# A two-block transformer kernel: the modulation's sums over partitions by a GpSimd all-reduce and a diagonal picked on VectorE, in place of TensorE's transposes and ones

## The chip, the cores and the metric

One core of one Trainium2 chip runs the program. The metric is device microseconds of one execution, the median of several runs; the profile is of one more execution, taken by the hardware profiler.

## What is computed

The reference is a chain of two transformer blocks on 256 tokens of width 1024, all in float32. The first has a forgetting attention with a convolution beside it and a SwiGLU; the second has two layers (a block attention, a differential attention), each with a SwiGLU, and each modulated by a vector `c`. The change touches only that modulation:

```python
def second_block(x, c, rel_bias, ada_w, ada_b, norm_g, ...):
    c_act = jax.nn.silu(c)
    for i in range(DEPTH_2):
        mod = (c_act @ ada_w[i] + ada_b[i])[:, None, :]
        sh_a, sc_a, g_a, sh_f, sc_f, g_f = jnp.split(mod, 6, axis=-1)
        h = rms_norm(x, norm_g[i, 0]) * (1.0 + sc_a) + sh_a
        ...
        x = x + g_a * rms_norm(y, norm_g[i, 1])
        h = rms_norm(x, norm_g[i, 2]) * (1.0 + sc_f) + sh_f
        x = x + g_f * rms_norm(swiglu_2(h, ffn_w_in[i], ffn_w_out[i]), norm_g[i, 3])
```

`mod` is a product of one row of 1024 numbers with a matrix of 1024 x 6144, twice: 48 MB of weights for one row.

## The kernel before, in words

**Products.** TensorE does every large product in three passes of fp32r: each weight unit of 128 x 512 is split into a high and a low part (`hi` or `wp` by ScalarE, `lo` or `wp` by VectorE, in `fill`, lines 316 to 345), each activation as well, and `triple` (line 370) issues high x high, high x low and low x high. A feed-forward step (`up`, `down`, lines 1089 to 1108) takes eight units up and four down; between them `activate` (line 1069) makes `ep` on VectorE (line 1073: silu times the other half, which lies in a PSUM bank), TensorE turns it (line 1078, matmul `bank<-ident,ep`), and ScalarE and VectorE split it into `pair`.

**The order.** The order of all engines is written by a planner that runs while the program is built (class `Order`, line 108). Its clock, `o.now`, advances with TensorE's matmuls. Small tasks are generators that yield the planner's time at which their next piece may be issued; `pump` runs those that are due between two matmuls. `Lane` (line 74) pins every instruction of an engine behind the one before it and charges it a planned cost. So each engine works through a fixed list, and an instruction that waits holds up everything behind it on its engine. While the chain from one stage to the next is under way (`chain`, line 526; its reciprocal square roots are `pow` on GpSimd, `rstd`, line 485), `o.urgent` is set and optional work is held back.

**The modulation.** `ada` (lines 630 to 661) spreads that product thinly over the first two thirds of the program. For each of 24 sums (two layers, six parts, two halves `cc` of 512 columns) GpSimd clears a tile `asum` (two of them, line 237), a DMA puts the bias into its first partition, and VectorE adds eight weight tiles, each scaled by its partition's number of `c_act` (line 656). What is left is a tile of 128 x 512 whose column sums over the 128 partitions are the result. `ada_finish` (lines 597 to 628) takes that sum:

- For the shifts and scales (`sh_a`, `sc_a`, `sh_f`, `sc_f`: 16 sums) the result must lie along partitions, as `fm`. TensorE turns the tile in four blocks into a bank (line 617), and VectorE sums over the free axis (line 622).
- For the gates (`g_a`, `g_f`: 8 sums) it must lie in every partition. ScalarE and VectorE split the tile (`split`, line 604, into a pair of the weight slots), TensorE multiplies both parts with a matrix of ones (lines 608 and 609), and VectorE multiplies the bank into `gain` (line 613).

The shifts and scales are needed by `evacuate` in the chains, the gates by `scaled_y` (line 533).

Of the kernel before, what the change touches and what calls it, by code (L numbers as in the profile page):

```python
# [5 lines left out]

# [5 lines left out]

# [3 lines left out]
OP = mybir.AluOpType  # L16
AX = mybir.AxisListType
# [3 lines left out]
P = 128  # L21
# [13 lines left out]
ADA_START, ADA_EARLY, ADA_LATE = 30.0, 5.5, 8.0  # L35
HEADS_1, HEADS_2 = 9.0, 2.0
PAD_END = 104
LAG = 3


# [33 lines left out]
class Lane:  # L74
# [7 lines left out]
    def __getattr__(self, name):  # L82
        fn = getattr(self.eng, name)

        def call(out, *args, after=0.0, **kw):
            self.order.pin(self, fn(out, *args, **kw))  # L86
            n = math.prod((args[0] if name == "reduce_sum" else out).shape[1:])
            aps = sum(hasattr(v, "shape") for v in (*args[1:], kw.get("scale"), kw.get("bias"), kw.get("accum_out")))
            cost = self.fixed + self.per * n
            src = args[0] if args and hasattr(args[0], "tensor") else None  # L90
            if src is not None and src.tensor.name.startswith("bank"):
                cost -= 0.042 if name == "activation" else 0.0
            elif name == "tensor_scalar":
                cost -= self.per * n / 2
            if name == "activation":
                cost += 0.093 * aps
            elif name in ("tensor_scalar", "scalar_tensor_tensor"):
                cost += 0.06 * (aps - (name[0] == "s"))
            if name == "activation" and args[1] not in (AF.Copy, AF.Square, AF.Identity, AF.Abs) and args[1] != self.table:
                self.table = args[1]  # L100
                cost += 1.3
            start = max(self.free, after, self.order.now)
            self.free = start + cost
            return self.free + 0.15
        return call
# [107 lines left out]
def block_kernel(ctx: ExitStack, tc: tile.TileContext, a: dict, onehot: bass.AP, out: bass.AP):  # L213
    nc = tc.nc
    o = Order(tc)
    A, V, G = o.A, o.V, o.G
# [6 lines left out]
    def ring(pool, name, n, shape, dtype=F32):  # L223
        return Ring([pool.tile(shape, dtype, name=f"{name}{i}") for i in range(n)])

    def small(name, shape, dtype=F32):
        return cst.tile(shape, dtype, name=name)

    banks = ring(psum, "bank", 8, [P, 512])
    raws = ring(cst, "raw", 3, [P, 2048])  # L230
    araws = ring(cst, "araw", 2, [P, 1024])
    slots = Ring([(small(f"hi{i}", [P, 512], F32R), small(f"lo{i}", [P, 512], F32R)) for i in range(16)])
    st = ring(cst, "st", 4, [P, 528])
# [3 lines left out]
    asum = ring(cst, "asum", 2, [P, 512])  # L237
# [26 lines left out]
    def ffn_stream(w_gu, w_dn, where):  # L264
# [3 lines left out]
        def up(s):  # L268
            for k0 in (0, 4):
                stream.append(Raw(gu[:, k0:k0 + 4, :, s * 256:(s + 1) * 256], 4, 512, where))  # L270

        def down(s):
            stream.append(Raw(dn[:, 2 * s:2 * s + 2, :], 2, 1024, where))
# [3 lines left out]
        for s in range(2, STEPS - 1):  # L277
            up(s)
            if s - 1 < STEPS - LAG:
                down(s - 1)  # L280
        up(STEPS - 1)
        for s in range(STEPS - LAG, STEPS):
            down(s)
# [63 lines left out]
    def split(hi, lo, src, after=0.0):  # L347
        t = A.activation(hi, src, AF.Copy, after=after)
        return V.tensor_sub(lo, src, hi.bitcast(F32), after=t)

    def take(n):
        got = [u for r in stream[pos["use"]:pos["use"] + n] for u in r.units]
        pos["use"] += n
        return got
# [27 lines left out]
    def product(ps, pair, h, ks, us, marks=None, first=True, last=True):  # L382

        n = len(us)
        for i, (k, u) in enumerate(zip(ks, us)):
            if marks is not None:
                o.wait(marks[h][k // 4])
            c = slice(h * P, (h + 1) * P)
            t = triple(ps, pair[0][:, k, c], pair[1][:, k, c], u, first and i == 0, last and i == n - 1)
        return t  # L390
# [71 lines left out]
    ident = small("ident", [P, P])  # L462
# [3 lines left out]
    ones_r = small("ones_r", [P, P], F32R)  # L466
# [130 lines left out]
    def ada_finish(l, what, cc, sums, r):  # L597
        yield r
        c = slice(cc * 512, (cc + 1) * 512)
        if what[0] == "g":  # L600
            yield from o.until(gated[l, what].load)
            pair = yield from o.get(slots)
            hv, lv = pair
            r = split(hv, lv, sums)
            asum.give(sums, r)
            yield r
            tp = yield from o.get(banks)
            o.mm(tp, ones_r, hv, True, False)
            r = o.mm(tp, ones_r, lv, False, True)
            slots.give(pair, r)  # L610
            yield r
            dst = gated[l, what].tile[:, c]
            r = V.tensor_mul(dst, dst, tp)
        else:
            tp = yield from o.get(banks)
            for j in range(4):
                r = o.tr(tp[:, j * P:(j + 1) * P], sums[:, j * P:(j + 1) * P], ident)
            asum.give(sums, r)
            yield r
            i = {"sh_a": 0, "sc_a": 1, "sh_f": 2, "sc_f": 3}[what]  # L620
            dst = fm[l][:, i, cc * 4:cc * 4 + 4]
            r = V.reduce_sum(dst, tp.rearrange("p (k c) -> p k c", c=P), axis=AX.X)
            if what[1] == "c":
                yield r
                g = vec["g", l, 0 if what == "sc_a" else 2][:, cc * 4:cc * 4 + 4]
                r = V.scalar_tensor_tensor(dst, dst, 1.0, g, op0=OP.add, op1=OP.mult)
        banks.give(tp, r)
        ada_done[l, what][cc].t = r

    def ada():  # L630
# [33 lines left out]
    def scope(**kinds):  # L664

        stack, got = ExitStack(), {}
        for name, (n, shape, dtype) in kinds.items():
            got[name] = ring(stack.enter_context(tc.tile_pool(name=name, bufs=1, reuse_waits="tile")), name, n, shape, dtype)
        return stack, got
# [87 lines left out]

    small("pad_end", [P, PAD_END])
    phase, sc = scope(qp=(4, [P, 4, 256], F32), gp=(8, [P, 512], F32),
# [195 lines left out]
    for k0 in (0, 4):  # L955
        for h in range(2):
            t = product(fb[h][:, :260], hT, h, range(k0, k0 + 4), us_f[k0:k0 + 4], hm, k0 == 0, k0 == 4)
# [50 lines left out]
    for n in range(2):  # L1008
        us = take(1)
        o.wait(ya_mark)  # L1010
        for h in range(2):
            ps = o.hold(banks)
            t = product(ps, yaT, h, range(4), us)
# [22 lines left out]
    for h in range(2):  # L1036
        for n in range(2):
            ps = o.hold(banks)
            t = product(ps, ybT, h, range(4), ub[n])
# [23 lines left out]
    def ffn(hm, gb, **kw):  # L1063
# [25 lines left out]
        def up(s, h):  # L1089
            if s not in us_of:  # L1090
                us_of[s] = take(2)
            act_mark[s, h] = Mark()
            ps = o.hold(banks)
            t = product(ps, hT, h, allk, us_of[s], hm)
            o.spawn(activate(s, h, ps), t)
# [14 lines left out]
        def downs(s):  # L1110
            for h in range(2):
                for n in range(2):
                    down(s, h, n)
# [6 lines left out]
        for s in range(2, STEPS - 1):  # L1120
            up(s, 0)
            up(s, 1)
            if s - 1 < STEPS - LAG:
                downs(s - 1)
        us_of[STEPS - 1] = take(2)
        for s in range(STEPS - LAG, STEPS):
            dn[s] = take(1)
        for h in range(2):
            up(STEPS - 1, h)
            o.spawn(chain(h, ys[h], gb, out_marks, **kw))  # L1130
            for s in range(STEPS - LAG, STEPS):
                for n in range(2):
# [237 lines left out]
```

## Time and profile before

| | us |
|---|---|
| median of 3 runs | 990.28 (989.15 to 990.47) |
| the profiled execution | 993.5 |
| its span, first to last instruction | 991.6 |
| TensorE busy | 975.9 of the span |
| VectorE busy | 739.2 |
| ScalarE busy | 605.2 |
| GpSimd busy | 35.2 |

Busy times are unions of an engine's instructions; matmuls are pipelined, and their ends are modelled, so two neighbours overlap. The distance from one start to the next is what a matmul costs in a row of matmuls. "Idle before" is what the engine stood still ahead of an instruction, with what released it. GpSimd's spans are rough.

### The profile page before, as it was taken

The page shows a single profiled execution, that of the slowest core. Times are in us where ns is not written, and L with a number is a line of the kernel's source. Part 1 is how long each engine was busy: PE and PEld are TensorE (multiplying, and loading weights), DVE is VectorE, ACT ScalarE, POOL GpSimd, SP SyncE. Part 2 cuts the span into 40 slices and gives each one's busy share as a digit, 9 for nine tenths or more (in the row PEclk, how much of TensorE's full clock was granted, in tenths as well). Part 3 has the DMA queues.
Part 4 walks back from the last instruction along what each step waited for, and adds up shares of the span by engine and source line. Part 5 has one row for each costly group of instructions (what it writes and reads, how often), then busy time and mean ns, then how long its engine had stood idle before and what let it go on. Part 6 is the DMA issues. An engine that isn't in the chain of part 4 may idle for free.

```text
span 991.6 us, 14032 instructions
## 1 busy us (share of the span) xinstructions
PE 975.9 (98%) x4814; PEld 808.5 (82%) x4814; DVE 739.2 (75%) x1469; ACT 605.2 (61%) x1286; POOL 35.2 (4%) x65
## 2 busy tenths in 40 slices
PE   7999999999999999999999999999999999999997
PEld 6888778888888888898788888888897888888886
DVE  5897879889888958887799888747765786464632
ACT  6746666774555537866685454637788795464531
POOL 1000000000000001000000000001000100000000
PEclk9999999999999999999999999999999999999999
DMA  6969778679989875775759989645542567646401
GB/s 217 361 202 308 254 263 271 218 231 319 363 287 326 294 257 189 253 258 173 233 187 313 369 274 314 231 138 194 176 163 86 172 206 253 211 157 207 163 33 43
DMA packets 143539, 227.19 MB, mean 229 GB/s; under 512 B 5991, under 2 KB 78932, under 8 KB 143468
## 3 DMA queue, kind: packets, MB, share of 16 engines
q1 hardware_dynamic: 143452, 226.30, 68.0%
q8 instruction: 37, 0.61, 0.2%
q14 instruction: 34, 0.28, 0.1%
q10 hardware_dynamic: 16, 0.00, 0.0%
HBM read 225.22 MB, written 2.63 MB: 230 GB/s over the span
## 4 chain that ended last, share of the span: by engine, by line
PE 92%; DMA 3%; issue 2%; DVE 1%; ACT 1%; SPq 0%; POOL 0%; DVEq 0%; POOLq 0%; ACTq 0%
PE bank L140 87%; PE bank L146 5%; DMA raw<-in_w_in_dram 1%; DMA raw<-in_ffn_w_in_dram 1%; DMA araw<-in_ada_w_dram 1%; DVE lo L86 1%; DMA ep<-in_norm_g_dram 0%; SPq L134 0%; DVE asum L86 0%; ACT hi L86 0%; DVE x L86 0%; ACT junk L86 0%; POOL tiny L86 0%; DVE wp L86 0%; DVE ep L86 0%
## 5 line engine op out<-in xcount | busy, mean ns | idle before, releaser
L86 DVE TENSOR_TENSOR lo<-raw,hi 128x512 fp32r<-128x512 f32 (+1 forms) x499 | 322.8, 676 | 41.4 <-ACT hi L86 40.1
L86 ACT ACTIVATE hi<-raw 128x512 fp32r<-128x512 f32 (+1 forms) x499 | 298.0, 620 | 61.4 <-PE bank L140 33.1
L140 PE MATMUL bank<-hi,hTh 128*128 128x512 f32 (+1 forms) x672 | 263.6, 392 | 0.0
L140 PE MATMUL bank<-hi,hTl 128*128 128x512 f32 (+1 forms) x672 | 262.6, 391 | 0.0
L140 PE MATMUL bank<-lo,hTh 128*128 128x512 f32 (+1 forms) x672 | 262.2, 390 | 0.3 <-DVE lo L86 0.3
L140 PE MATMUL bank<-hi,pair 128*128 128x512 f32 x524 | 173.9, 396 | 0.0
L86 DVE SCALAR_TENSOR_TENSOR asum<-araw,c_act,asum 128x512 f32<-128x512 f32 x192 | 143.0, 745 | 7.5 <-DMA araw<-in_ada_w_dram 6.5
L140 PEld LDWEIGHTS bank<-hi,hTl 128*128 128x128 f32 x672 | 126.9, 189 | 25.5 <-issue 1.7
L140 PEld LDWEIGHTS bank<-lo,hTh 128*128 128x128 f32 x672 | 127.0, 189 | 24.0 <-DVE lo L86 0.6
L140 PEld LDWEIGHTS bank<-hi,hTh 128*128 128x128 f32 x672 | 127.1, 189 | 23.3 <-issue 0.2
L140 PE MATMUL bank<-wp,hTh 128*128 128x512 f32 x384 | 119.1, 391 | 0.0
L140 PEld LDWEIGHTS bank<-hi,pair 128*128 128x128 f32 x524 | 98.1, 189 | 19.5
L86 ACT ACTIVATE wp<-raw 128x512 fp32r<-128x512 f32 x145 | 88.5, 629 | 26.0 <-PE bank L140 16.7
L140 PE MATMUL bank<-lo,pair 128*128 128x512 f32 x262 | 103.9, 396 | 0.0
L86 ACT ACTIVATE ep<-bank 128x256 f32<-128x256 f32 x66 | 25.3, 383 | 125.8 <-PE bank L140 125.4
L86 DVE TENSOR_TENSOR wp<-raw,wp 128x512 fp32r<-128x512 f32 x145 | 94.9, 684 | 9.1 <-ACT wp L86 8.3
L140 PEld LDWEIGHTS bank<-wp,hTh 128*128 128x128 f32 x384 | 71.8, 188 | 15.0
L86 DVE TENSOR_TENSOR ep<-ep,bank 128x256 f32<-128x256 f32 x70 | 29.1, 416 | 70.8 <-ACT ep L86 70.2
L140 PE MATMUL bank<-wp,pair 128*128 128x512 f32 x294 | 76.7, 395 | 0.0
L140 PE MATMUL bank<-wp,hTl 128*128 128x512 f32 x192 | 75.1, 391 | 0.0
L140 PEld LDWEIGHTS bank<-wp,pair 128*128 128x128 f32 x294 | 54.3, 188 | 10.9
L86 ACT ACTIVATE pair<-bank 128x256 fp32r<-128x256 f32 (+1 forms) x74 | 28.8, 389 | 53.7 <-PE bank L146 42.4
(128 smaller groups left out, 952.4 us busy)
## 6 DMA issues: line engine op xcount, KB each, us to landing
araw<-in_ada_w_dram SPq DMA_DIRECT2D x96, 512.0 KB
raw<-in_ffn_w_in_dram SPq DMA_DIRECT2D x88, 512.0 KB
raw<-in_w_gate_up_dram SPq DMA_DIRECT2D x44, 512.0 KB
raw<-in_ffn_w_out_dram SPq DMA_DIRECT2D x22, 1024.0 KB
raw<-in_w_in_dram SPq DMA_DIRECT2D x18, 1024.0 KB
raw<-in_moba_w_qkv_dram SPq DMA_DIRECT2D x12, 1024.0 KB
raw<-in_diff_w_qkv_dram SPq DMA_DIRECT2D x12, 1024.0 KB
raw<-in_w_down_dram SPq DMA_DIRECT2D x11, 1024.0 KB
```

Source lines behind the costliest of these rows:

```text
L86: self.order.pin(self, fn(out, *args, **kw))
L140: self.pin(self.pe, self.nc.tensor.matmul(out, lhsT, rhs, start=start, stop=stop, skip_group_check=shared))
L146: self.pin(self.pe, self.nc.tensor.transpose(out, src, ident))
```

## The change

The cross-partition sum leaves TensorE. GpSimd's `partition_all_reduce` writes the column sums of the tile into every partition of a tile of the ring `st` (four tiles, line 233). For the gates VectorE multiplies that into `gain`. For the shifts and scales four VectorE instructions, one for each block of 128 columns, multiply the block with the identity and accumulate along the row, which leaves in partition p the sum of column p. The planner charges the new instruction 8.0 us, and neither it nor the VectorE instructions behind it are issued while `o.urgent` is set.

```diff
-from concourse import mybir
+from concourse import bass_isa, mybir
...
+ALL_REDUCE = 8.0
...
             cost = self.fixed + self.per * n
             src = args[0] if args and hasattr(args[0], "tensor") else None
+            if name == "partition_all_reduce":
+                cost = ALL_REDUCE
...
     def ada_finish(l, what, cc, sums, r):
         yield r
         c = slice(cc * 512, (cc + 1) * 512)
+        while o.urgent:
+            yield o.now + 0.2
+        total = yield from o.get(st)
+        t = total[:, :512]
+        r = G.partition_all_reduce(t, sums, channels=P, reduce_op=bass_isa.ReduceOp.add)
+        asum.give(sums, r)
+        yield r
+        while o.urgent:
+            yield o.now + 0.2
         if what[0] == "g":
             yield from o.until(gated[l, what].load)
-            pair = yield from o.get(slots)
-            hv, lv = pair
-            r = split(hv, lv, sums)
-            asum.give(sums, r)
-            yield r
-            tp = yield from o.get(banks)
-            o.mm(tp, ones_r, hv, True, False)
-            r = o.mm(tp, ones_r, lv, False, True)
-            slots.give(pair, r)
-            yield r
             dst = gated[l, what].tile[:, c]
-            r = V.tensor_mul(dst, dst, tp)
+            r = V.tensor_mul(dst, dst, t)
         else:
-            tp = yield from o.get(banks)
-            for j in range(4):
-                r = o.tr(tp[:, j * P:(j + 1) * P], sums[:, j * P:(j + 1) * P], ident)
-            asum.give(sums, r)
-            yield r
             i = {"sh_a": 0, "sc_a": 1, "sh_f": 2, "sc_f": 3}[what]
             dst = fm[l][:, i, cc * 4:cc * 4 + 4]
-            r = V.reduce_sum(dst, tp.rearrange("p (k c) -> p k c", c=P), axis=AX.X)
+            for j in range(4):
+                r = V.scalar_tensor_tensor(t[:, j * P:(j + 1) * P], t[:, j * P:(j + 1) * P], 1.0, ident, op0=OP.mult, op1=OP.mult,
+                                           accum_out=dst[:, j:j + 1])
...
-        banks.give(tp, r)
+        st.give(total, r)
         ada_done[l, what][cc].t = r
```

On GpSimd, behind the fifth of the 24 sums, where the first projection's four `pow` stand (`tiny<-tiny,mhalf`; `MEMSET asum` clears a sum's tile), the order before is:

```order
L86 MEMSET asum_121 128x512
L86 MEMSET asum_122 128x512
L86 TENSOR_TENSOR tiny_147<-tiny_148,mhalf 128x1
L86 TENSOR_TENSOR tiny_150<-tiny_151,mhalf 128x1
L86 TENSOR_TENSOR tiny_153<-tiny_154,mhalf 128x1
L86 TENSOR_TENSOR tiny_156<-tiny_157,mhalf 128x1
L86 MEMSET asum_121 128x512
```

Nothing stands there but the clears and the `pow`. Now there is also the all-reduce (`ISA st<-asum`, and an `ISA` without tiles, which loads another library of GpSimd code):

```order
L87 MEMSET asum_122 128x512
L87 ISA st_108<-asum_121 128x512
L87 ISA
L87 TENSOR_TENSOR tiny_147<-tiny_148,mhalf 128x1
L87 TENSOR_TENSOR tiny_150<-tiny_151,mhalf 128x1
L87 TENSOR_TENSOR tiny_153<-tiny_154,mhalf 128x1
L87 TENSOR_TENSOR tiny_156<-tiny_157,mhalf 128x1
L87 MEMSET asum_121 128x512
L87 ISA
L87 ISA st_111<-asum_122 128x512
```

Each of the 24 sums has such an all-reduce, and for all but the last two a clear of the same tile waits behind it; a library load stands at each of the eight changes between all-reduces and `pow`, in front of the next instruction that needs it.

On VectorE, in the first modulated feed-forward (the sixth sum, `asum_122`), what stands behind the sum's last addition is now:

```order
L87 SCALAR_TENSOR_TENSOR asum_122<-araw_75,c_act,asum_122 128x512
L87 TENSOR_TENSOR lo_99<-raw_71,hi_98 128x512
L87 TENSOR_TENSOR lo_101<-raw_71,hi_100 128x512
L87 TENSOR_TENSOR lo_103<-raw_71,hi_102 128x512
L87 TENSOR_TENSOR ep_118<-ep_118,bank_65 128x256
L87 TENSOR_TENSOR lo_105<-raw_71,hi_104 128x512
L87 TENSOR_TENSOR lo_107<-raw_72,hi_106 128x512
```

The weight splits `lo<-raw,hi` read two SBUF tiles each; `ep`, which TensorE turns next, is one of a list in which they come first. The sum's diagonal stands sixteen instructions behind that last addition:

```order
L87 TENSOR_TENSOR ep_115<-ep_115,bank_69 128x256
L87 SCALAR_TENSOR_TENSOR asum_121<-araw_75,c_act,asum_121 128x512
L87 SCALAR_TENSOR_TENSOR st_111,fm_191<-st_111,ident 128x128 x4
L87 TENSOR_TENSOR pair_166<-bank_63,pair_166 128x256
L87 TENSOR_TENSOR wp_1634<-raw_73,wp_1633 128x512
```

Before, one `TENSOR_REDUCE fm<-bank` stood four rows behind the sum's last addition. On TensorE the rows `bank<-ident,asum` (16 groups of four) and `bank<-hi,ones_r`, `bank<-lo,ones_r` (8 of each) are gone, and nothing has come in their place.

## Rows read from the trace of the kernel before

**Rows 1.** The page: busy time by engine, and the granted TensorE clock in 40 slices.

```profile
PE 975.9 (98%) x4814; PEld 808.5 (82%) x4814; DVE 739.2 (75%) x1469; ACT 605.2 (61%) x1286; POOL 35.2 (4%) x65
...
PEclk9999999999999999999999999999999999999999
```

**Rows 2.** The page: the chain that ended last, shares by engine.

```profile
PE 92%; DMA 3%; issue 2%; DVE 1%; ACT 1%; SPq 0%; POOL 0%; DVEq 0%; POOLq 0%; ACTq 0%
```

**Rows 3.** Busy time by stretch: stretch, its length, then each engine's.

```profile
40.00:200.00 160.00, 159.66 (x769) 128.74 (x768) 137.03 (x279) 101.97 (x210) 5.83 (x13) 1.00 0.77 259
200.00:372.00 172.00, 171.99 (x793) 140.66 (x792) 146.04 (x255) 89.76 (x172) 4.83 (x10) 1.00 0.88 297
372.00:480.00 108.00, 108.00 (x632) 94.87 (x631) 86.65 (x181) 78.64 (x175) 4.42 (x7) 1.00 0.67 221
480.00:640.00 160.00, 157.57 (x714) 128.71 (x713) 134.05 (x240) 93.08 (x182) 5.93 (x10) 0.99 0.82 278
```

**Rows 4.** Groups by line: busy us, mean ns, idle before (the parts removed).

```profile
L86 DVE TENSOR_REDUCE fm<-bank 128x4 f32<-128x512 f32 x16 | 11.0, 685 | 2.4 <-PE bank L146 2.3
...
L146 PE MATMUL bank<-ident,asum 128*128 128x128 f32 x64 | 9.6, 273 | 0.0
...
L86 DVE TENSOR_TENSOR lo<-asum,hi 128x512 fp32r<-128x512 f32 x8 | 5.5, 692 | 4.5 <-ACT hi L86 4.5
...
L140 PE MATMUL bank<-hi,ones_r 128*128 128x512 f32 x8 | 3.5, 439 | 0.0
```

**Rows 5.** Timeline of PE: start, us, instruction (a shift's four turns; a gate's ones).

```profile
217.86 0.39 PE L140 MATMUL bank<-lo,pair 128*128 128x512 f32 x1
...
218.31 0.60 PE L146 MATMUL bank<-ident,asum 128*128 128x128 f32 x4
...
219.21 0.63 PE L140 MATMUL bank<-hi,pair 128*128 128x512 f32 x2
...
277.81 0.39 PE L140 MATMUL bank<-hi,ones_r 128*128 128x512 f32 x1
...
278.27 0.40 PE L140 MATMUL bank<-hi,hTh 128*128 128x512 f32 x1
```

**Rows 6.** Groups on DVE, shapes apart: the nearest instructions to a diagonal's.

```profile
L86 DVE DVE_READ_ACCUMULATOR2_ANT tiny<- 128x1 f32 x64 | 5.3, 82 | 0.0
...
L86 DVE SCALAR_TENSOR_TENSOR ep<-ep,tiny,ep 128x128 f32<-128x128 f32 x8 | 2.8, 346 | 0.2
```

**Rows 7.** Groups on POOL, shapes apart.

```profile
L86 POOL TENSOR_TENSOR tiny<-tiny,mhalf 128x1 f32<-128x1 f32 x22 | 15.3, 694 | 454.1 <-DVE tiny L86 454.1
L86 POOL MEMSET asum<- 128x512 f32 x24 | 12.6, 525 | 353.9 <-PE bank L146 196.4 <-DVE lo L86 120.4 <-DVE ep L86 18.8
L86 POOL TENSOR_TENSOR tiny<-tiny,mhalf 128x4 f32<-128x4 f32 x4 | 4.3, 1080 | 85.1 <-DVE tiny L86 79.9 <-ACT wp L86 5.1
```

**Rows 8.** Timelines of POOL and DVE around three of the `pow`.

```profile
183.63 0.55 POOL L86 TENSOR_TENSOR tiny<-tiny,mhalf 128x1 f32<-128x1 f32 x1 [43.92 <-DVE tiny L86]
187.43 0.93 POOL L86 TENSOR_TENSOR tiny<-tiny,mhalf 128x1 f32<-128x1 f32 x1 [3.24 <-DVE tiny L86]
...
183.47 0.69 DVE L86 TENSOR_TENSOR ch<-bank,gain 128x512 f32<-128x512 f32 x1
...
187.27 0.68 DVE L86 TENSOR_TENSOR lo<-raw,hi 128x512 fp32r<-128x512 f32 x1
...
498.75 0.68 DVE L86 TENSOR_TENSOR wp<-raw,wp 128x512 fp32r<-128x512 f32 x1
...
498.38 0.55 POOL L86 TENSOR_TENSOR tiny<-tiny,mhalf 128x1 f32<-128x1 f32 x1 [8.24 <-DVE tiny L86]
```

**Rows 9.** Timelines of DVE and PE: an activation made, and turned.

```profile
248.34 0.41 DVE L86 TENSOR_TENSOR ep<-ep,bank 128x256 f32<-128x256 f32 x1
...
248.81 0.44 PE L146 MATMUL bank<-ident,ep 128*128 128x128 f32 x2
```

**Rows 10.** Groups on DVE in the stretch of 200 to 372 us.

```profile
L86 DVE TENSOR_TENSOR ep<-ep,bank 128x256 f32<-128x256 f32 x21 | 8.7, 415 | 9.4 <-ACT ep L86 9.4
```

## The prediction

> **What bounds the kernel now.** [...] The chain that ended last is TensorE for 92% [rows 2]. Then the stretches in which the 24 sums are taken: from 40 to 640 us TensorE is busy 597.2 of 600 us, so a matmul taken away there shortens the program. In the same four stretches VectorE is busy 86, 85, 80 and 84% [rows 3]: not the bound, but with only 15% to spare, a loss on it is won back slowly.
>
> **What it removes.** A shift's four turns: from one matmul to the next but three around them TensorE takes 219.21 - 217.86 = 1.35 us, in which four large matmuls also start; those cost 0.23 each, as the two of the ones do (278.27 - 277.81 = 0.46) [rows 5]. That leaves 0.43 for the turns, 16 x 0.43 = 6.9 us. A gate's ones: 8 x 0.46 = 3.7 us. Together **10.6 us of TensorE**, on the path. Off it go 11.0 us of VectorE's row sums and 5.5 of its splits [rows 4] and as many splits of ScalarE's, which is far from full [rows 1].
>
> **What it adds on VectorE.** A diagonal takes four instructions of 128 x 128 with two SBUF inputs and an accumulator to read; the nearest rows are 346 ns for such a multiply and 82 for the read [rows 6], at most 4 x 0.43 = 1.7 us where one sum took 0.69. So 16 x 1.0 = 16 us more, 5.5 less for the splits: some 10 us in 600. The price lies between nothing (VectorE has the room) and all of it (TensorE reads what VectorE has just made: `ep` ends at 248.75, and its turn starts at 248.81 [rows 9]); I take **2 us**, near the lower end, since the order was written with these instructions in it.
>
> **What it adds on GpSimd.** 24 all-reduces of 128 x 512. No row has one. The nearest below is the clear of as many columns, 0.53 us; the nearest above is `pow`, whose step from one column to four, (1080 - 694) / 3 = 129 ns a column, would give 66 us [rows 7]. The order gives it room: 13 to 17 VectorE instructions stand between nearly every sum's last addition and what reads its all-reduce (sixteen in the order shown), and with its idle time VectorE spends 172 / 255 = 0.67 us on each [rows 3]; so 9 us pass, at the least, before anything on VectorE waits. I take 8 us, the figure the order was laid out for; it is no row's, and what the sum needs of it is first whether it is under 9. Under 9, and if VectorE went on undisturbed, the whole would be 10.6 - 2 = 8.6 us faster. The `pow` of the chains are not behind an all-reduce in time: GpSimd stood idle for 43.9 us ahead of the first of them [rows 8]. The library loads lie in that idle time; ahead of an all-reduce a load would have to take over 1 us to be felt, four times.
>
> **What decides it.** Does a GpSimd instruction that reads SBUF for microseconds let VectorE work? Two sorts of `pow` in the trace say how the two engines share. At 183.63 the `pow` runs beside a multiply that reads a bank and one SBUF tile, and takes 0.55 us. At 187.43 it runs beside a split `lo<-raw,hi`, which reads two SBUF tiles and ends at 187.95; now it takes 0.93 and ends 0.41 later, at 188.36 [rows 8]. So GpSimd's read of a single column waited until the whole VectorE instruction was through: the two do not share column by column, one has the port and the other stands. In the other direction the rows say less: at 498.75 a split starts 0.37 us into a `pow` of 0.55 and takes its usual 0.68 [rows 8], so GpSimd gives the port back at the latest after two thirds of its instruction. A `pow` of one column reads for too short a time to be seen holding anything; an all-reduce reads 512. The hold is thus between nothing and, by two thirds, 0.67 x 8 = 5.4 us. I take 5.4, because the pattern that the rows do show is the exclusive one, and an instruction that sums as it reads has no reason to be done reading early.
>
> What 5.4 us of a standing VectorE cost: behind the sum's last addition stand splits with two SBUF inputs, and `ep` behind them in the list. TensorE's weights are split well ahead, but `ep` is not: it is used 0.06 us after it is made [rows 9]. There are 21 `ep` in 172 us [rows 10], one every 8.2, so the next comes on average 4.1 us after the hold begins, late by the hold less what VectorE wins back until then, 15% of 4.1 = 0.6. Off goes another 0.7, while VectorE finishes the instruction that has the port, and 0.5 for those `ep` that are made earlier than needed. 5.4 - 1.8 = 3.6 us for each of 24, **86 us**.
>
> **The sum**, against the profiled execution's own 993.5 us: 993.5 - 10.6 + 2 + 86 = 1070.9. That execution is 3.2 us above the median shown; against the median it is 990.3 - 10.6 + 2 + 86 = **1068 us**.
>
> **The rivals.**
> - *No hold that matters.* The instruction takes its 512 columns in quickly, or GpSimd is served between VectorE's instructions, as the `pow` at 187.43 was; VectorE never stands. For it: no row shows VectorE held, and clears of 128 x 512 cost VectorE nothing visible (though they do not read). Then 990.3 - 8.6 = 982 us, faster. It decides below a hold of 1.8 + 8.6 / 24 = 2.2 us; just about there the two cancel.
> - *The port is held for the whole instruction.* 24 x (8.0 - 1.8) = 149 us, 990.3 - 8.6 + 149 = 1131 us. The split at 498.75, which started before the `pow` had ended and lost nothing [rows 8], speaks against it, if weakly. [...]
> - *The instruction is longer than its room.* Each microsecond beyond 9 makes the diagonal wait, and VectorE with it, 24 us a microsecond. Of each wait 1.1 us is again won back or covered. At 14 us, 24 x (5 - 1.1) = 94, and without any hold 990.3 - 8.6 + 94 = 1076; gain and loss cancel at 9 + 1.1 + 8.6 / 24 = 10.5. Late clears then also hold the bias DMAs on SP's queue, with the weights behind them. The `pow` price of 66 us would add 24 x (57 - 1.1) = 1,340. [...]
>
> That the change does not do what it says is excluded on TensorE: the turns and the ones are gone from its list.
>
> **How the numbers follow.** About 0.2%, 2 us, is what a measurement of this kernel tells from no change. Forecast (a hold of 2.6 to 6 us): 0.38. No hold that matters: 0.36. Whole instruction: 0.12. Longer than its room: 0.10. Holds that just cancel the gain: 0.04. So faster 0.36, same 0.04, slower 0.60. The forecast's own range is 1001 to 1083 us (holds of 2.6 and 6). The range that is to hold 8 of 10 must take in the rival on the other side, 982 with the whole price of the diagonals' 0 to 10 us open, so from 977; above, it goes to 1128, which leaves out most of the whole-instruction case and the longest instructions.
>
> **What would show it.** If I am right: the group of `lo<-raw,hi`, 0.68 us each now, has members of several microseconds, or idle time of that size ahead of them, 24 times, where GpSimd's all-reduce runs; TensorE's turns of `ep` wait for VectorE about 3.6 us after most sums; TensorE's busy sum falls by some 11 us while the span grows. The step on the hold is wrong if splits keep 0.68 us and a 0.60 us pitch through an all-reduce; the step on 8 us is wrong if the all-reduce takes over 9, and then VectorE waits at the diagonal, named as released by GpSimd; the step on the libraries is wrong if a `pow` or an all-reduce stands idle behind a load. The prediction as a whole is wrong if TensorE's matmuls stay back to back through the sums: then the time is near 982.

## The result, and the profile after

The changed kernel takes **997.44 us** (median of 8 runs, 991.98 to 1003.24) beside 991.38 us of the kernel before, measured next to it (8 runs, 989.15 to 992.87). The ratio is 1.0063, 95% interval 1.0043 to 1.0084: slower by 0.6%, some 6 us. The prediction said slower, and 1068 us: the direction held, the size was wrong by 71 us. The profiled execution took 1000.14 us, its span is 998.4. Two executions in the experiments ran at a lower granted clock (0.558 for one of twelve in halves, 0.852 for one of the kernel before beside them); the ratios leave them out.

The page of the changed kernel, busy line, granted clock and the chain by engine:

```profile
PE 969.6 (97%) x4734; PEld 798.9 (80%) x4734; DVE 775.0 (78%) x1573; ACT 599.7 (60%) x1278; POOL 126.5 (13%) x89
...
PEclk9999999999999999999999999999999999999999
...
PE 69%; DVE 17%; DMA 7%; issue 4%; ACT 1%; POOL 0%; SPq 0%; DVEq 0%; POOLq 0%; ACTq 0%
```

TensorE lost its 80 instructions, and its clock in the 40 slices is as before [rows 1]; its mean is 0.997 in both. VectorE grew by 36 us of busy time, and its share of the chain rose from 1 to 17% [rows 2]. Its groups, and GpSimd's new one (busy us, mean ns of one, idle before):

```profile
L87 DVE TENSOR_TENSOR lo<-raw,hi 128x512 fp32r<-128x512 f32 (+1 forms) x499 | 344.5, 719 | 37.8 <-ACT hi L87 36.6
...
L87 DVE SCALAR_TENSOR_TENSOR asum<-araw,c_act,asum 128x512 f32<-128x512 f32 x192 | 150.9, 786 | 10.7 <-DMA araw<-in_ada_w_dram 10.1
...
L87 DVE TENSOR_TENSOR wp<-raw,wp 128x512 fp32r<-128x512 f32 x145 | 103.3, 742 | 7.6 <-ACT wp L87 7.4
...
L87 POOL PARTITION_ALL_REDUCE st<-asum x24 | 91.2, 3800 | 409.2 <-DVE asum L87 323.6 <-issue 45.2 <-DVE tiny L87 25.7
...
L87 DVE SCALAR_TENSOR_TENSOR st<-st,ident 128x128 f32<-128x128 f32 x64 | 14.7, 283 | 0.0
```

The 64 diagonal instructions are only 14.7 us. Most of the rest of the growth is in instructions that the change did not touch: the splits and the additions `asum`, all of 128 x 512 with two SBUF tiles to read, have a higher mean than where no all-reduce runs beside them (the first experiment shows these groups). Which ones? The tile view of `asum` gives minimum, median and maximum:

```profile
L87 DVE SCALAR_TENSOR_TENSOR asum<-araw,c_act,asum x192: 733/744/2728, 42.2 to 651.7; 128x512 f32<-128x512 f32 x192
...
L87 POOL PARTITION_ALL_REDUCE st<-asum x24: 3234/3547/5839, 65.9 to 652.5; - x24
```

The median addition still takes 744 ns; single ones take up to 2.7 us. And the all-reduce, of which no row stood ahead of the prediction, takes **3.23 us** at the least. One of the 24, in the timeline (GpSimd, then VectorE; start, us, instruction):

```profile
291.59 3.23 POOL L87 PARTITION_ALL_REDUCE st<-asum  x1 [17.72 <-DVE asum L87]
```

```profile
291.41 0.42 DVE L87 TENSOR_TENSOR ep<-ep,bank 128x256 f32<-128x256 f32 x1
291.74 2.64 DVE L87 TENSOR_TENSOR lo<-raw,hi 128x512 fp32r<-128x512 f32 x1
```

The split begins at 291.74 and ends at 294.38; its own work is 0.68 us, so it could begin it only at 293.70. That is 2.1 us after the all-reduce began, and 1.1 before it ended: VectorE goes on after 65% of the instruction. This time is called the hold below. A second case gives the same (2.27 - 0.68 us from 558.12 on, 2.11 us after 557.60), and shows what is not held:

```profile
557.60 3.23 POOL L87 PARTITION_ALL_REDUCE st<-asum  x1 [15.11 <-DVE asum L87]
```

```profile
557.77 0.43 DVE L87 TENSOR_TENSOR pair<-bank,pair 128x256 fp32r<-128x256 f32 x1 [0.27 <-ACT pair L87]
558.12 2.27 DVE L87 TENSOR_TENSOR lo<-raw,hi 128x512 fp32r<-128x512 f32 x1
```

`pair<-bank,pair`, which reads one bank and one SBUF tile, takes 0.43 us inside the all-reduce, as in the kernel before (70 of them, mean 423 ns); the next instruction, with two SBUF tiles, stands.

How the hold reaches TensorE: at 538.31 an all-reduce of 3.59 us begins, and VectorE's list goes on so, five instructions to the next `ep`; then TensorE:

```profile
538.72 2.73 DVE L87 TENSOR_TENSOR lo<-raw,hi 128x512 fp32r<-128x512 f32 x1
541.37 0.74 DVE L87 SCALAR_TENSOR_TENSOR asum<-araw,c_act,asum 128x512 f32<-128x512 f32 x1
542.04 0.68 DVE L87 TENSOR_TENSOR lo<-raw,hi 128x512 fp32r<-128x512 f32 x1
542.64 0.74 DVE L87 SCALAR_TENSOR_TENSOR asum<-araw,c_act,asum 128x512 f32<-128x512 f32 x1
543.30 0.41 DVE L87 TENSOR_TENSOR ep<-ep,bank 128x256 f32<-128x256 f32 x1
```

```profile
543.77 0.44 PE L149 MATMUL bank<-ident,ep 128*128 128x128 f32 x2 [2.03 <-DVE ep L87]
```

The split at 538.72 stood for 2.05 us, VectorE then worked back to back, `ep` came that much later, and TensorE stood for 2.03 us. Nothing was won back on the way. Over the program, TensorE's waits for it (us in total, times, longest):

```profile
PE bank L149 <- DVE ep L87: 12.2, 16, 2.0
```

Before, that row read:

```profile
PE bank L146 <- DVE ep L86: 0.2, 1, 0.2
```

The list of the weight loads' own waits has another 17.2 us for `ep`, 29.4 with both.

### The profile page after: what moved, and what is told of

It reads as the page before. It is cut to its first block, busy times and chain, and to the rows that moved or that the text cites. A ratio compares the mean times of both kernels' runs of the same rounds, so it can differ in the third digit from the quotient of the medians.

```text
span 998.4 us, 14020 instructions
## 1 busy us (share of the span) xinstructions
PE 969.6 (97%) x4734; PEld 798.9 (80%) x4734; DVE 775.0 (78%) x1573; ACT 599.7 (60%) x1278; POOL 126.5 (13%) x89
## 4 chain that ended last, share of the span: by engine, by line
PE 69%; DVE 17%; DMA 7%; issue 4%; ACT 1%; POOL 0%; SPq 0%; DVEq 0%; POOLq 0%; ACTq 0%
PE bank L143 65%; DVE asum L87 6%; DMA araw<-in_ada_w_dram 6%; DVE lo L87 5%; PE bank L149 4%; DVE wp L87 2%; DVE ep L87 1%; DMA raw<-in_ffn_w_in_dram 1%; DVE gp L87 1%; DMA raw<-in_w_in_dram 1%; DVE pair L87 1%; ACT hi L87 1%; DVE hTl L87 0%; DVE ch L87 0%; DVE x L87 0%
## 5 line engine op out<-in xcount | busy, mean ns | idle before, releaser
L87 DVE TENSOR_TENSOR lo<-raw,hi 128x512 fp32r<-128x512 f32 (+1 forms) x499 | 344.5, 719 | 37.8 <-ACT hi L87 36.6
L87 ACT ACTIVATE hi<-raw 128x512 fp32r<-128x512 f32 (+1 forms) x499 | 297.5, 620 | 59.4 <-PE bank L143 28.8
L87 DVE SCALAR_TENSOR_TENSOR asum<-araw,c_act,asum 128x512 f32<-128x512 f32 x192 | 150.9, 786 | 10.7 <-DMA araw<-in_ada_w_dram 10.1
L87 POOL PARTITION_ALL_REDUCE st<-asum x24 | 91.2, 3800 | 409.2 <-DVE asum L87 323.6
L143 PE MATMUL bank<-wp,hTh 128*128 128x512 f32 x392 | 121.8, 391 | 0.0
L87 DVE TENSOR_TENSOR wp<-raw,wp 128x512 fp32r<-128x512 f32 x145 | 103.3, 742 | 7.6 <-ACT wp L87 7.4
L143 PE MATMUL bank<-wp,pair 128*128 128x512 f32 x282 | 74.4, 400 | 0.0
L87 POOL TENSOR_TENSOR tiny<-tiny,mhalf 128x1 f32<-128x1 f32 (+1 forms) x26 | 19.7, 759 | 408.7 <-DVE tiny L87 403.5
```

The lines of the kernel that those rows point to most:

```text
L143: self.pin(self.pe, self.nc.tensor.matmul(out, lhsT, rhs, start=start, stop=stop, skip_group_check=shared))
```

## The experiments

Ten kernels were run, each beside the kernel before. The last column is VectorE's busy time in the profiled execution. The change and the kernels marked with a star have the same list of VectorE instructions, so there this column tells directly how long VectorE stood, as the difference to the first kernel's 740.1. The expected texts count each standing instruction's extra length instead (39.8 us for the change, where the busy times give 34.9).

| kernel | us, median | ratio to before, 95% interval | VectorE busy |
|---|---|---|---|
| the change * | 997.44 | 1.0063 [1.0043, 1.0084] | 775.0 |
| 1: nothing read * | 980.25 | 0.9893 [0.9875, 0.9910] | 740.1 |
| 2: before, with the all-reduce | 1008.61 | 1.0163 [1.0144, 1.0183] | 776.5 |
| 3: room of 3.3 us | 1002.15 | 1.0107 [1.0091, 1.0123] | 770.2 |
| 4: the planner told of the hold | 979.71 | 0.9879 [0.9864, 0.9894] | 760.4 |
| 5: all-reduce twice * | 1053.05 | 1.0619 [1.0599, 1.0639] | 817.8 |
| 6: in halves * | 990.71 | 0.9993 [0.9978, 1.0007] | 767.2 |
| 7: gates only | 989.40 | 0.9980 [0.9969, 0.9991] | 744.1 |
| 8: before, with the planner's push alone | 989.28 | 0.9981 [0.9971, 0.9991] | 737.7 |
| 9: in quarters * | 986.97 | 0.9960 [0.9945, 0.9975] | 756.5 |
| 10: told, and in halves | 979.33 | 0.9876 [0.9857, 0.9895] | 753.3 |

### 1 and 2: the change without the hold, the hold without the change

The first kernel keeps the change's order on every engine and clears the tile where the all-reduce stood; the modulation's sums are left out of the computation. The second is the kernel before, with an all-reduce behind each sum's last addition, written into a buffer of the ring `ch` from which nobody reads it (`...` stands for lines left out).

```diff
-        r = G.partition_all_reduce(t, sums, channels=P, reduce_op=bass_isa.ReduceOp.add)
+        r = G.memset(t, 0.0) + ALL_REDUCE - 0.46
+        G.free += ALL_REDUCE - 0.46
```

```diff
+    scrap = ch.free[2][1]
...
     def ada_finish(l, what, cc, sums, r):
         yield r
+        o.pin(G, nc.gpsimd.partition_all_reduce(scrap, sums, channels=P, reduce_op=bass_isa.ReduceOp.add))
```

> The all-reduce is replaced by a clear of the same st tile, which writes 128 x 512 and reads nothing, with the same planned cost of 8.0 us: the order on TensorE, VectorE, ScalarE and SyncE is the changed kernel's, row for row; the sums are left out. Theory (VectorE stands while GpSimd reads): no VectorE instruction over 1.3 us, TensorE's waits for ep fall back to some 2 us, and the time is the kernel before less 8 to 11 us, 980 to 984. Rival A (the order laid out for 8 us of room, and the 64 diagonal instructions on VectorE): those are still there, so 995 to 999. Rival B (library loads and the GpSimd queue): the eight loads are gone too, so this run alone does not separate it from the theory; the times of the all-reduces and of pow in the other runs do.

> The kernel before, with one all-reduce of each finished sum added into a tile that nobody reads, and no other change: same order on all other engines, TensorE's turns and ones kept. Theory: 24 VectorE instructions stand 1.0 to 2.1 us over their usual time, some 40 us in all, and TensorE waits for ep some 15 us more: 1003 to 1010 against 991. Rival A: within 2 us of the kernel before. Rival B (loads and queue): the pow would start late behind loads; if the hold costs nothing, at most 2 us.

Without the all-reduce the kernel takes 980.25 us, 11.0 less than before. Its busy line, and its groups: the same instructions are back at the lengths of the kernel before, with the 64 diagonals still in the list:

```profile
PE 964.7 (98%) x4734; PEld 798.7 (81%) x4734; DVE 740.1 (76%) x1573; ACT 599.1 (61%) x1278; POOL 46.5 (5%) x89
...
L87 DVE TENSOR_TENSOR lo<-raw,hi 128x512 fp32r<-128x512 f32 (+1 forms) x499 | 323.8, 677 | 39.1 <-ACT hi L87 37.6
...
L87 DVE SCALAR_TENSOR_TENSOR asum<-araw,c_act,asum 128x512 f32<-128x512 f32 x192 | 143.3, 746 | 8.8 <-DMA araw<-in_ada_w_dram 7.9
...
L87 DVE TENSOR_TENSOR wp<-raw,wp 128x512 fp32r<-128x512 f32 x145 | 94.9, 686 | 8.6 <-ACT wp L87 8.4
...
L87 DVE SCALAR_TENSOR_TENSOR st<-st,ident 128x128 f32<-128x128 f32 x64 | 14.7, 285 | 0.0
```

```profile
PE bank L149 <- DVE ep L87: 1.6, 3, 0.6
```

So the change without its all-reduces gains 11 us, and the all-reduces cost 997.44 - 980.25 = 17.2 us, **0.72 us each**. The first kernel lacks the library loads too, and its clear takes only 0.53 us, so by itself it does not part the hold from the loads or from a late all-reduce. For the hold speak the waits: in the change no `pow` waits without a named releaser, and TensorE's two queues wait 29.4 us for `ep`, here 4.6. Kernels 5, 6 and 9 then vary the hold with the order kept.

The kernel before, given 24 all-reduces and nothing else, loses 17.4 us. The two agree, with one reserve: in the second one part of the loss is another thing. There an all-reduce ends at 377.16 + 3.23 = 380.39, and a chain's `pow`, with a library load in front, begins at 387.84:

```profile
377.16 3.23 POOL L600 PARTITION_ALL_REDUCE ch<-asum  x1 [18.97 <-DVE asum L86]
387.84 0.59 POOL L86 TENSOR_TENSOR tiny<-tiny,mhalf 128x1 f32<-128x1 f32 x1 [7.45 <-issue]
```

```profile
388.46 1.41 DVE L86 SCALAR_TENSOR_TENSOR x<-ch,tiny,x 128x512 f32<-128x512 f32 x2 [4.23 <-POOL tiny L86]
```

GpSimd waits 7.45 us for nothing that the profile shows, and VectorE 4.23 us for the `pow`, in the middle of a chain. If TensorE loses as much, the hold's share of the 17.4 is nearer 13, an estimate (17.4 - 4.2).

### 3: less room for the all-reduce

The planner charges it 3.3 us, close to its true length, in place of 8.0.

```diff
-ALL_REDUCE = 8.0
+ALL_REDUCE = 3.3
```

> The changed kernel with ALL_REDUCE = 3.3 in place of 8.0, near the 3.2 us that the instruction takes undisturbed; diagonals and clears are ordered earlier. Theory: the holds are all there (some 40 us), and the diagonal now comes when the all-reduce may have been late by 0.4 to 2.6 us, so 996 to 1003, no better. Rival A (room too wide): better by most of the loss, 984 to 990.

It is 4.4 us slower than the change (by the ratios), though VectorE is busy less. Three waits in its list:

```profile
PEld bank L149 <- DVE ch L87: 7.4, 3, 6.7
...
POOL tiny L87 <- issue: 7.2, 1, 7.2
...
DVE x L87 <- POOL tiny L87: 6.4, 1, 6.4
```

A `pow` of a chain waits 7.2 us in the same way, VectorE 6.4 for the `pow`, and TensorE up to 6.7 behind it. The 8.0 was too long as a cost, but with it no `pow` of a chain waited so; a true cost alone is no improvement. That the wait is the library load, which stands there in the list, is a reading: the profile names no releaser.

### 4 and 8: the planner told of the hold, and its control

One line behind the all-reduce tells the planner that VectorE is away for 2 us, so that it puts what TensorE needs next ahead of the splits. The control has the same push behind each finished sum in the kernel before, without any all-reduce.

```diff
         r = G.partition_all_reduce(t, sums, channels=P, reduce_op=bass_isa.ReduceOp.add)
+        V.free = max(V.free, o.now) + 2.0
```

```diff
     def ada_finish(l, what, cc, sums, r):
         yield r
+        V.free = max(V.free, o.now) + 2.0
```

> The changed kernel with one line more: at an all-reduce the planner counts VectorE as taken for 2.0 us, so that what reads VectorE's results is ordered later on TensorE. Theory: VectorE stands as before (some 40 us in 24 pieces), but TensorE's waits for ep, 29 us now by both of its queues, fall under 12, and the time comes to 983 to 990, below both kernels. Rival A or B: VectorE's work is only pushed back, no gain, 996 to 1002.

> The kernel before, with nothing of the change, but with the planner's VectorE pushed back by 2.0 us at each finished sum, as in the kernel that was told of the hold. Theory (that kernel's 980 us come from keeping holds out of the way): here there is no hold to keep out of the way, so no gain: 989 to 995 us. Rival (the push finds a better order by itself): 978 to 984 us.

Told of the hold, the change takes 979.71 us, 1.2% under the kernel before, which **beats both kernels**. The control gains 0.2%: in the kernel before, the push by itself is worth 2 of the 12 us. The push in the changed order without all-reduces was not run, so how much of the 12 us comes from the other order there stays open. One of the all-reduces:

```profile
256.49 4.81 POOL L87 PARTITION_ALL_REDUCE st<-asum  x1 [11.79 <-DVE asum L87]
```

```profile
256.32 1.89 DVE L87 TENSOR_TENSOR wp<-raw,wp 128x512 fp32r<-128x512 f32 x3
260.85 0.42 DVE L87 TENSOR_TENSOR ep<-ep,bank 128x256 f32<-128x256 f32 x1 [2.65 <-ACT ep L87]
```

Three splits run through at 0.6 us each and end at 258.21; the all-reduce ends at 261.30, largely beside the 2.65 us in which VectorE waits for ScalarE anyway. It took 4.81 instead of 3.23 us, and 3.09 of them lie behind the splits: that it in turn waited for them is read from this. VectorE's busy time still holds some of the hold (760.4), but the wait of TensorE's turns for `ep` is down to this:

```profile
PE bank L149 <- DVE ep L87: 0.3, 1, 0.3
```

With the weight loads it is 1.5 us, in place of 29.4. So VectorE still stands some 20 us (760.4 - 740.1, an estimate, since its list is in another order), and it costs nothing that can be seen: the time is that of the kernel without all-reduces (980.25).

### 5: the all-reduce twice

The same all-reduce is issued twice in a row, with the planner's clock left as in the change.

> The all-reduce is issued twice in a row into the same tile (48 instead of 24); the order of TensorE, VectorE, ScalarE and SyncE is that of the change. Theory (each all-reduce holds VectorE's two-input work for about 2.0 of its 3.23 us, and each hold costs about 0.7 us of the end): VectorE instructions that stand go from 24 with 39.8 us in sum to some 45 with 70 to 80, and the time goes up by 24 x 0.7 = 17 us or more, since the second hold finds the lead already spent: 1010 to 1030 us. Rival (the 17 us between the change and the kernel with the all-reduce left out are not the hold but the waits behind a late all-reduce, or the library loads): the second all-reduce adds only where GpSimd is behind, 997 to 1003 us.

The time is 1053 us: well above the range that theory gave, and far from the rival. VectorE stood 77.7 us (817.8 - 740.1) in place of 34.9, 42.8 us more, and the time went up by 55.6. Its busy line:

```profile
PE 987.4 (94%) x4734; PEld 810.3 (77%) x4734; DVE 817.8 (78%) x1573; ACT 601.7 (57%) x1278; POOL 206.9 (20%) x113
```

The span is 1051.4 us, so TensorE is idle for 64.0 us, 35 more than in the change (998.4 - 969.6 = 28.8), and busy for 18 more with the same instructions. Of the idle time 25 us are longer waits of its matmuls for `ep` (37.7 in place of 12.7): the second hold of a pair finds less lead, that is less time between the making of `ep` and its use, than the first. Some 8 us are not VectorE's hold but GpSimd's own list. In a chain a `pow` begins only after 9.0 us of idle time behind a pair, and TensorE waits 3.2 us there. And a clear in an `st` tile, which TensorE's next turns need, stands behind the pair that begins at 65.6:

```profile
73.73 0.18 POOL L87 MEMSET st<- 128x8 f32 x1
73.97 1.06 PE L149 MATMUL bank<-ident,st 128*66 128x128 f32 x4 [5.04 <-POOL st L87]
```

So the rival's waits behind GpSimd are there, but they are a small part of the loss. The longer busy time fits TensorE's clock. In stretches of 4 us from 64 to 84 us (busy times of PE, PEld, DVE, ACT, POOL, then the granted clock):

```profile
64.00:68.00 4.00, 4.00 (x20) 3.28 (x19) 3.96 (x8) 1.45 (x4) 2.43 (x1) 1.00 0.37 100
68.00:72.00 4.00, 0.92 (x4) 0.40 (x3) 2.76 (x5) 1.38 (x3) 3.90 (x2) 1.00 0.76 272
72.00:76.00 4.00, 2.04 (x10) 1.59 (x10) 0.94 (x2) 0.51 (x1) 1.91 (x2) 0.62 0.07 25
76.00:80.00 4.00, 4.00 (x12) 3.18 (x11) 2.40 (x5) 1.38 (x3) 0.56 (x2) 0.53 0.48 143
80.00:84.00 4.00, 4.00 (x21) 3.19 (x20) 3.01 (x14) 2.48 (x5) 0.00 (x0) 1.00 0.48 158
```

From 68 to 72 us TensorE is busy 0.92 of 4 us, because of that wait, and in the next two stretches the granted clock is 0.62 and 0.53: at 0.53 it does 12 matmuls in 4 us, where it did 20 at 1.00. The mean clock of this run is 0.979, of the changed kernel's 0.997; 0.018 of 1051 us is some 19 us, at most, close to the 18 above.

### 6, 9 and 10: in pieces

The all-reduce goes as two of 256 columns, as four of 128, and as two with the planner told. The planner is charged once.

```diff
-        r = G.partition_all_reduce(t, sums, channels=P, reduce_op=bass_isa.ReduceOp.add)
+        g0 = G.free
+        G.partition_all_reduce(t[:, :256], sums[:, :256], channels=P, reduce_op=bass_isa.ReduceOp.add)
+        G.free = g0
+        r = G.partition_all_reduce(t[:, 256:], sums[:, 256:], channels=P, reduce_op=bass_isa.ReduceOp.add)
```

> Each all-reduce of 512 columns is issued as two of 256; same order on the other engines. If the hold goes with the columns read (two thirds of the instruction), each half takes about 1.6 to 1.9 us, VectorE stands twice for about 1 us, between which it can get one instruction done, and the sum of the standing stays near 40 us: 990 to 1002 us. If the instruction has a large fixed part in which the port is held, each half takes well over 2 us, the sum of the standing rises above 55 us, and the time above 1005 us.

> Each all-reduce is issued as four of 128 columns; same order on the other engines. From 3.23 us for 512 columns and 1.79 for 256, a quarter should take about 1.1 us and hold VectorE about 0.45. Theory (a hold costs only what it has above a lead of about 0.5 to 1 us that VectorE wins back between two pieces): nearly no price is left, 980 to 986 us, against 980.25 with the all-reduce left out. Rival (the price goes with the sum of the standing, whatever its pieces: 17 us for 39.8, 10 for 29.4): the four quarters stand for 20 to 30 us in sum, 988 to 992 us.

> The planner is told of the hold (VectorE pushed back by 2.0 us behind each all-reduce), and each all-reduce is issued as two of 256. Theory: what was left of the price with the planner told (16 that stand, 25.1 us in sum) falls too: 975 to 979 us. Rival (nothing of the price was left there, the two pieces only add fixed time on GpSimd): 979 to 982 us, as told alone.

The halves take 990.71 us, no different from before. A half on GpSimd, and VectorE beside it:

```profile
287.48 1.79 POOL L87 PARTITION_ALL_REDUCE st<-asum  x1 [16.82 <-DVE asum L87]
```

```profile
287.64 1.49 DVE L87 TENSOR_TENSOR lo<-raw,hi 128x512 fp32r<-128x512 f32 x1
```

The quarters take 986.97 us, and there the same pair of rows reads:

```profile
342.79 1.07 POOL L87 PARTITION_ALL_REDUCE st<-asum  x1 [11.28 <-DVE asum L87]
```

```profile
342.94 0.91 DVE L87 TENSOR_TENSOR wp<-raw,wp 128x512 fp32r<-128x512 f32 x1
```

The all-reduce takes 1.07, 1.79 and 3.23 us for 128, 256 and 512 columns: 5.6 ns a column and 0.35 fixed. Worked out as above, VectorE goes on 0.38, 0.97 and 2.1 us after the start: 4.4 to 4.6 ns for each further column. So the hold goes with the columns, and it is no fixed share of the instruction: 36, 54 and 65%. In the pieces VectorE stands for 27.1 (halves) and 16.4 us (quarters) in place of 34.9, since it gets an instruction in between (in the quarters a split at 343.78 takes its 0.68 us, and the addition behind it stands again, 1.00 us in place of 0.74), and the price falls to 10.5 and 6.7 us (990.71 and 986.97 less 980.25).

The quarters ended just above the theory's 986 and below the rival's 988. By the price alone they speak for the rival: 0.49, 0.39 and 0.41 us for each microsecond that VectorE stands, in whole, halves and quarters. The rival took the standing of quarters too long (20 to 30 us against 16.4). But a part of the 6.7 us is GpSimd's own list again, the same clear and a `pow` of a chain:

```profile
PE bank L149 <- POOL st L87: 2.2, 1, 2.2
...
POOL tiny L87 <- issue: 8.7, 1, 8.7
```

Behind that `pow` TensorE waits 1.4 us more. With both taken off some 3 us are left for 16.4 us of standing, an estimate, and that is nearer to the theory. In the halves TensorE waits 1.5 us for the clear; in the change a weight load waits 1.7 us for it. So the price falls when VectorE stands less; whether a short hold is free stays open. Told and in halves gives 979.33 us, the same as told alone (979.71): the rival's value. With that order the pieces save nothing.

### 7: the gates alone

The 16 shifts and scales go back to TensorE's turns and VectorE's row sums; the 8 gates keep the all-reduce.

> Only the 8 gates use the all-reduce; the 16 shifts and scales are turned by TensorE and summed by VectorE as before. Theory: gain 8 x 0.46 = 3.7 us of TensorE, price 8 x 0.72 = 5.8 us: 991.2 + 2 = 993 us (990 to 997), with about 8 VectorE instructions that stand, 13 us in sum. Rival (the price is in the diagonals of the 16 shifts and scales, not in the hold): 987.5 us or less.

989.40 us: below the theory's 990 to 997, above the rival's 987.5. The rival's diagonals cost nothing in the first kernel either, so it is the theory's price for a gate that was too high. VectorE is busy 744.1 us, and the turns are back, so the 3.7 us of the ones are set against less than 0.72 for each hold: (3.7 - 1.5) / 8 = 0.3, taking 1.5 us from the difference to before, 990.91. That the price of a hold differs by place is what the timelines show too (2.03 us at 543.77, nothing at others); that the gates' places are the cheaper ones is a reading, not shown.

## Why the prediction was wrong in size

**TensorE's gain, 10.6 us:** right. The kernel that reads nothing gains 11.0, with TensorE's busy time down by 11.2 (975.9 to 964.7). In the changed kernel itself that sum fell by only 6.3 (to 969.6), not by the 11 that was given as a sign; the rest was not traced.

**The diagonals, 2 us of 0 to 10:** at the lower end. The same 11.0 us contain them, so they cost nothing that can be seen. One is 283 ns, not 346.

**The length of the all-reduce, 8 us:** this is the step that failed. The prediction took "8 us, the figure the order was laid out for", noting that it was no row's. It is a planner's constant, with room in it; measured, it is 3.23 us undisturbed, 3.8 on average, within the bounds (0.53 to 66) but far from what was taken. An allowance was used as a size. The term of 86 us, 3.6 for each sum, came out as 17.2, 0.72 for each.

**Two thirds of it hold VectorE:** the number was right, with luck. It is 2.1 of 3.23 us, 65%. The row gave two thirds only as an upper end, for a `pow` of one column, and the pieces show that the share changes with the columns (36, 54 and 65%). 'Port' is the prediction's word for what the two engines share: the rows and runs show only which instruction stands, and for how long. The exclusive pattern, one engine standing while the other works, was right both ways: GpSimd waits as well, by this reading. At 436.19 its all-reduce lasts 5.84 us; splits run back to back on VectorE until 438.93, then VectorE waits 0.44 us for ScalarE, and the next split stands. From 438.93 to its end the all-reduce takes 3.1 us, near its 3.23:

```profile
436.19 5.84 POOL L87 PARTITION_ALL_REDUCE st<-asum  x1 [12.69 <-DVE asum L87]
```

```profile
435.84 3.09 DVE L87 TENSOR_TENSOR lo<-raw,hi 128x512 fp32r<-128x512 f32 x5
439.38 2.21 DVE L87 TENSOR_TENSOR lo<-raw,hi 128x512 fp32r<-128x512 f32 x1 [0.44 <-ACT hi L87]
```

**What a hold costs, hold less 1.8 us:** too kind. By that formula a hold of 2.1 us costs 0.3, 7 us in all, and with 8.6 off the change would have been even. Measured, it is 0.72 each: 1.4 us are covered, not 1.8. TensorE's turns waited for `ep` 16 times for 0.8 us on average, not 3.6 us after most sums. The form fails on the halves as well: two holds of 0.97 us, less 1.8, would cost 0.14 a sum and 3 us in all, where 10.5 were measured, 1.5 of them the wait for the clear.

With the price of the second kernel, which was measured apart from the change, the sum is 991.4 - 11.0 + 17.4 = 997.8 us, against 997.44; so close an agreement is partly luck, since by the estimate above some 4 of the 17.4 are the late `pow`. (The 17.2 gives the time by its making.) The prediction's formula with 3.23 us put in would have given 990: the wrong length made the forecast too slow, the generous cover would have made it too fast. So that the direction held is partly luck too: with the right length the prediction would have said no change. The break-even point stated, a hold of 2.2 us, lay just above the measured hold of 2.1, which is why a chance of 0.04 for "same" was small for a case that came out at 0.6%.

**The library loads lie in idle time:** held for the change, and only for its order. In it no `pow` waits without a releaser in the list of waits; in the second, third, fifth and ninth kernel one each does, for 7.45, 7.2, 9.0 and 8.7 us (that it is for the load is the reading above).

**The rivals:** the hold for the whole instruction is excluded (65%). "Longer than its room" is excluded: the longest lasts 5.84 us. "No hold that matters" is excluded as a mechanism, but 980 us, where it would have led, is what the kernel reaches once the order knows of the hold.

## What to carry to other kernels

In these runs the all-reduce is a wait on VectorE's list of 0.38, 0.97 and 2.1 us for 128, 256 and 512 columns, paid by the first VectorE instruction with two SBUF inputs. What decides its price is which instruction stands behind that one (997.44 us in one order, 979.71 in another), so plan it like work on both engines, with what TensorE needs next ahead of it. Look at GpSimd's own list as well: with the all-reduce twice, TensorE waited 5.0 us for a clear behind it, and a `pow` began after 9.0 us of idle time. When the duration of a new instruction is in no trace, a planner's constant for it is a room and not a duration: carry the range through to the end, and see whether the break-even lies in it. A share taken from a short instruction need not carry over to a long one either: here it went from 36 to 65% with the columns.

## What had not been expected of the hardware

- An all-reduce took longer where VectorE's instructions with two SBUF inputs ran back to back beside it: 5.84 us in place of 3.23 at 436.19, beside five splits, and 4.81 at 256.49 in the fourth kernel, beside three.
- Between an all-reduce and the next `pow` GpSimd stood idle for 7.2 to 9.0 us in four of the kernels, with no releaser in the profile, over ten times the `pow`'s own 0.59.
- The changed kernel's eight runs spread over 11 us (991.98 to 1003.24), those of the kernel before beside it over 4. In the kernel told of the hold four runs spread over 2.5 (977.95 to 980.41), with the all-reduce twice over 3.7. What makes the change's time vary was not tried.
